# Attention on TensorE: the order of transposes and products with the values, one group at a time and two at a time

## The chip, the cores and the metric

One core of one Trainium2 chip runs the whole program. The metric is the device time of one execution in microseconds (us). TensorE does matmuls and transposes, ScalarE copies and exponentials, VectorE the softmax arithmetic, GpSimd (POOL) elementwise sums, and SyncE (SP) issues the DMA transfers.

## What is computed

A decoder layer over 1024 positions: a convolution group, an attention group and an RWKV-7 group share one input projection; one output projection and a gated MLP follow. The change lies in the attention, which has 8 query heads (2 key/value heads, 4 queries each), 128 queries at a time, and three branches. Cut to the two that matter here:

```python
def one_block(c):                       # 128 queries
    ...
    s = jnp.einsum('bqgrd,bgqnld->bgrqnl', qc, kg).astype(f32) * scale
    ps = masked_softmax(s, msel, (-2, -1))
    o_sel = jnp.einsum('bgrqnl,bgqnld->bqgrd', ps.astype(vg.dtype), vg)
    ...
    s = jnp.einsum('bqgrd,bkgd->bgrqk', qc, kwc).astype(f32) * scale
    pw = masked_softmax(s, mwin, (-1,))
    o_win = jnp.einsum('bgrqk,bkgd->bqgrd', pw.astype(vwc.dtype), vwc)
    return gc[..., 0:1] * o_cmp + gc[..., 1:2] * o_sel + gc[..., 2:3] * o_win
```

The third branch, `o_cmp`, attends to compressed blocks and is small.

## The kernel before

The kernel is traced in program order and a planner then orders the instructions of every engine ahead of time: earlier work of the program goes first when it is ready in the planner's own timeline, later work fills the gaps. Each engine then runs its list strictly in that order and waits for semaphores.

`attn_tile(i)` handles one tile of 128 queries; eight tiles run in the order 7, 6, 5, 4, 0, 3, 2, 1. For each of two branches (`br` 2 is the window of up to 640 keys, `br` 1 is all keys up to the tile's last, under the selection mask) and each of four heads `r` (two key/value heads `g` at once) it does this:

- scores, L897 and L898: a high and a low part of the keys, in pieces of at most 512 keys, into a PSUM bank of the tag `mm` (3 banks);
- L901 adds the mask and takes the minimum (VectorE), into a buffer `pp` (6 of them); L908 the exponential (ScalarE); L909, L910 and L915 the scale by the reciprocal sum and the gate (VectorE);
- then in groups of up to 256 keys: up to four transposes of 128 x 128 (L922) into a PSUM bank of the tag `tr` (2 banks); one copy of the bank to a buffer `pT` by ScalarE (L925); up to four products with the values (L930), each for one key/value head, into 64 of the 128 partitions of the tile's accumulator `av` (1 bank).

After the window branch `cmp_av` adds the compressed branch (L866, L868, L869); at the end L936 copies `av` out and L937 stores it. Beside the attention run the RWKV chain (`rwkv_chain`, L595, L601, L612, L615), which the program gives a high priority, sums of the MLP's down weights on POOL (L949 to L952), and towards the end the load and splitting of the output projection's weights (`wout_load`, L968, L971, with `split` at L120 and L121). Behind it comes the output projection (`out_tile`, matmuls at L229, loads at L988 and L992).

## Time and profile before

| | us |
|---|---|
| median of 3 runs | 1487.43 |
| the runs | 1487.43, 1487.57, 1479.73 |
| the profiled execution | 1479.4 |
| its span, first to last instruction | 1477.5 |
| the attention's stretch in it | 396.0 to 704.5 |

In the views below a row of the timeline is: start in us, length in us, engine, line, operation, out<-in, form (rows and columns of the array, then partitions x elements), count, and in brackets the idle time of the engine before it with what ended it. PE is TensorE's matmuls, PEld its weight loads, DVE VectorE, ACT ScalarE. Matmuls are pipelined, so the lengths of neighbours overlap: what one costs is read from start to start.

### The profile page before, as it was taken

To read this page: it belongs to the slowest core of one execution; us is meant where nothing else is said; L and a number is where in the kernel's file an instruction comes from. 1 tells how busy PE (TensorE), PEld (TensorE's weight loads), DVE (VectorE), ACT (ScalarE), POOL (GpSimd) and SP (SyncE) were. 2 spreads that over 40 slices of the span, in tenths; PEclk is the share of its full clock that TensorE was granted. 3 is DMA by queue.
4 is the path that set the end of the run, shared out by engine and by line. 5 is a ranking of instruction groups with operands and counts; after the bars stand their busy time and mean duration, and the time that the engine had idled before them with its cause. 6 is when DMAs were issued, how large, how long until landed. Compare 5 with 4: busy or idle time off the path is not lost.

```text
span 1477.5 us, 22767 instructions
## 1 busy us (share of the span) xinstructions
PE 1388.7 (94%) x7897; PEld 1095.2 (74%) x7897; DVE 1002.7 (68%) x2187; ACT 686.9 (46%) x1377; POOL 499.2 (34%) x607
## 2 busy tenths in 40 slices
PE   6999589998899999999799899999999999999997
PEld 5887457776677676766588677888788788888886
DVE  6347594454868778798257867676775776666685
ACT  5441245624456665678223533343343333445463
POOL 1002996921144066220000144443444442113310
PEclk9999888999899999999899999999999999999999
DMA  6133133436514254542722123332332334986533
GB/s 185 40 107 82 44 103 111 142 84 179 153 33 139 78 154 125 181 150 81 240 89 83 43 93 93 108 107 70 104 113 93 108 100 162 388 280 216 188 92 114
DMA packets 206679, 186.69 MB, mean 126 GB/s; under 512 B 56355, under 2 KB 145764, under 8 KB 206564
## 3 DMA queue, kind: packets, MB, share of 16 engines
q1 hardware_dynamic: 206564, 185.24, 40.3%
q8 instruction: 62, 1.02, 0.3%
q14 instruction: 53, 0.43, 0.1%
HBM read 126.99 MB, written 58.20 MB: 125 GB/s over the span
## 4 chain that ended last, share of the span: by engine, by line
PE 79%; DVE 8%; POOL 4%; DMA 3%; ACT 2%; issue 2%; SPq 1%; ACTq 0%; DVEq 0%; POOLq 0%
PE gb L229 13%; PE mm L229 12%; PE rw L229 10%; PE ga L229 9%; PE gc L229 8%; PE tr L229 5%; PE tr L922 5%; PE av L930 4%; PE mm L897 2%; PE mm L898 2%; POOL sT L534 1%; POOL sx L532 1%; DVE pp L901 1%; POOL cacc L279 1%; DVE pp L915 1%
## 5 line engine op out<-in xcount | busy, mean ns | idle before, releaser
L229 PE MATMUL mm<-hT,whi 128*128 128x512 f32 x608 | 200.3, 409 | 19.6 <-DVE ev L690 14.8
L229 PEld LDWEIGHTS mm<-hT,whi 128*128 128x128 f32 x608 | 115.7, 193 | 48.9 <-ACT whi L120 20.2
L229 PE MATMUL mm<-hT,wlo 128*128 128x512 f32 x304 | 123.0, 407 | 1.9 <-DVE wlo L121 1.9
L925 ACT ACTIVATE pT<-tr 128x512 f32<-128x512 f32 (+1 forms) x152 | 79.9, 536 | 60.6 <-PE tr L922 59.2
L930 PE MATMUL av<-pT,V 128*64 128x128 f32 x1056 | 96.0, 287 | 1.5 <-ACT pT L925 1.5
L1076 POOL TENSOR_TENSOR S<-wraw,wr 128x512 f32<-128x512 f32 x22 | 28.5, 1296 | 192.8 <-DVE or L107 91.1
L922 PE MATMUL tr<-idn,pp 128*128 128x128 f32 x528 | 90.3, 289 | 1.8 <-DVE pp L915 1.8
L279 POOL TENSOR_TENSOR cacc<-cacc,ctap 128x512 f32<-128x512 f32 x60 | 85.1, 1429 | 12.7 <-ACT ctap L278 12.4
L121 DVE TENSOR_TENSOR sp<-rb,sp 128x512 fp32r<-128x512 f32 x66 | 55.6, 842 | 49.4 <-ACT sp L120 49.4
L229 PE MATMUL rw<-woh,mix 128*128 128x512 f32 x240 | 79.5, 407 | 9.0 <-ACT mix L120 9.0
L229 PE MATMUL rw<-sp,sp 128*128 128x512 f32 x330 | 86.0, 389 | 0.0
L229 PE MATMUL tr<-sp,sp 128*128 128x512 f32 x330 | 85.9, 389 | 0.0
L897 PE MATMUL mm<-KH,QS 128*128 128x512 f32 (+2 forms) x192 | 77.7, 411 | 3.1 <-DVE mx L901 2.8
L930 PEld LDWEIGHTS av<-pT,V 128*64 128x64 f32 x1056 | 59.2, 136 | 28.3 <-issue 13.7
L922 PEld LDWEIGHTS tr<-idn,pp 128*128 128x128 f32 x528 | 55.9, 141 | 30.5 <-issue 29.1
L915 DVE TENSOR_SCALAR pp<-pp,sm 128x640 f32<-128x640 f32 (+7 forms) x128 | 76.5, 638 | 0.9
L120 ACT ACTIVATE sp<-rb 128x512 fp32r<-128x512 f32 x66 | 41.6, 630 | 74.1 <-PE tr L229 36.5
L121 DVE TENSOR_TENSOR sp<-b,sp 128x512 fp32r<-128x512 f32 x88 | 72.1, 827 | 5.2 <-ACT sp L120 5.0
L229 PEld LDWEIGHTS mm<-hT,wlo 128*128 128x128 f32 x304 | 58.5, 193 | 18.1 <-DVE wlo L121 3.8
L229 PEld LDWEIGHTS tr<-sp,sp 128*128 128x128 f32 x330 | 61.9, 188 | 12.9
L229 PEld LDWEIGHTS rw<-sp,sp 128*128 128x128 f32 x330 | 61.9, 188 | 12.9
L532 POOL TENSOR_TENSOR sx<-sN,sT 128x60 f32<-128x60 f32 (+24 forms) x124 | 48.0, 387 | 63.0 <-DMA sN<-dn 54.9
(455 smaller groups left out, 3648.8 us busy)
## 6 DMA issues: line engine op xcount, KB each, us to landing
wr<-in_ffn_w_gate_dram SPq DMA_DIRECT2D x44, 256.0 KB
wraw<-in_ffn_w_up_dram SPq DMA_DIRECT2D x44, 256.0 KB
pdS<-prod SPq DMA_DIRECT2D x44, 256.0 KB
b<-pdS SPq DMA_DIRECT2D x44, 256.0 KB
rb<-tdT SPq DMA_DIRECT2D x44, 256.0 KB
pdA<-prod SPq DMA_DIRECT2D x33, 256.0 KB
b<-pdA SPq DMA_DIRECT2D x33, 256.0 KB
wraw<-in_w_in_dram SPq DMA_DIRECT2D x30, 256.0 KB
```

Source lines behind the costliest of these rows:

```text
L120: self.nc.scalar.activation(hi, src, AF.Copy)
L121: getattr(self.nc, eng).tensor_tensor(lo, src, hi.bitcast(F32), op=ALU.subtract)
L229: mm = lambda l, r, **k: self.nc.tensor.matmul(out, l, r, skip_group_check=more, **k)
L279: nc.gpsimd.tensor_tensor(t[:, o:o + 512], t[:, o:o + 512], z, op=ALU.add)
L532: v_.tensor_tensor(x, N[:, q, q + 1:32].unsqueeze(2).to_broadcast([P, n, w]), Tm[:, q, 0:w].unsqueeze(1).to_broadcast([P, n, w]), op=ALU.mult)
L897: pe.matmul(pts[g][:, 0:n], QS[:, r, g, :], KH[g][hf][:, ks], start=True, stop=False)
L898: pe.matmul(pts[g][:, 0:n], QS[:, r, g, :], KL[g][hf][:, ks], start=False, stop=True)
L915: v.tensor_scalar(Ps[g], Ps[g], sm[:, g:g + 1], None, op0=ALU.mult)
L922: pe.transpose(pt[:, o:o + P], Ps[g][:, kt * P:kt * P + P], self.idn)
L925: s.activation(pT[:, 0:n], pt[:, 0:n], AF.Copy)
L930: pe.matmul(av[g * 64:g * 64 + 64, r * P:r * P + P], self.V[kk // 2][:, kk % 2, vo + g * 64:vo + g * 64 + 64], pT[:, o:o + P], start=first ...
L1076: gp.tensor_tensor(t, x, y, op=op)
```

## The change

Products are no longer traced behind the evacuation of their own group. They are put on a list; when the list holds two groups, the products of both are traced. `issue_after(x)` puts the TensorE instructions traced in its block behind `x` in TensorE's queue: an order of issue, no wait for `x` to finish. The products stand behind the last transpose of the second group, and every group's transposes stand behind the last product traced before them (`av_ins`, kept across tiles). The list is emptied at the end of a tile. What is computed, and the number of instructions, stays the same.

```diff
         first = [True, True]
+        pend = []
+        after = lambda ins: self.tc.issue_after(ins) if ins is not None else nullcontext()
+
+        def products():
+
+            for br, r, lo_k, W, vo, kts, pT, ti in pend:
+                with after(pend[-1][-1]):
+                    for kt in kts:
+                        kk = lo_k // P + kt
+                        for g in range(2):
+                            o = (kt - kts[0]) * 256 + g * P
+                            self.av_ins = pe.matmul(av[g * 64:g * 64 + 64, r * P:r * P + P],
+                                                    self.V[kk // 2][:, kk % 2, vo + g * 64:vo + g * 64 + 64], pT[:, o:o + P],
+                                                    start=first[g], stop=br == 1 and r == 3 and kt == W // P - 1).ins
+                            first[g] = False
+            del pend[:]
...
                     pt = self.bank("tr")
-                    for kt in kts:
-                        for g in range(2):
-                            o = (kt - k2) * 256 + g * P
-                            pe.transpose(pt[:, o:o + P], Ps[g][:, kt * P:kt * P + P], self.idn)
+                    with after(self.av_ins):
+                        for kt in kts:
+                            for g in range(2):
+                                o = (kt - k2) * 256 + g * P
+                                t = pe.transpose(pt[:, o:o + P], Ps[g][:, kt * P:kt * P + P], self.idn)
                     pT = self.xt([P, 512], "pT")
                     n = len(kts) * 256
                     s.activation(pT[:, 0:n], pt[:, 0:n], AF.Copy)
-                    for kt in kts:
-                        kk = lo_k // P + kt
-                        for g in range(2):
-                            o = (kt - k2) * 256 + g * P
-                            pe.matmul(av[g * 64:g * 64 + 64, r * P:r * P + P], self.V[kk // 2][:, kk % 2, vo + g * 64:vo + g * 64 + 64], pT[:, o:o + P],
-                                      start=first[g], stop=br == 1 and r == 3 and kt == W // P - 1)
-                            first[g] = False
+                    pend.append((br, r, lo_k, W, vo, kts, pT, t.ins))
+                    if len(pend) == 2:
+                        products()
             if br == 2:
                 cmp_av()
+        products()
```

In `build`, `self.av_ins = None` is set ahead of the loop over the tiles.

## Rows read from the trace of the kernel before

**Rows 1.** The page: each engine's busy time, share of the span, instructions.

```profile
PE 1388.7 (94%) x7897; PEld 1095.2 (74%) x7897; DVE 1002.7 (68%) x2187; ACT 686.9 (46%) x1377; POOL 499.2 (34%) x607
```

**Rows 2.** Stretch table: length, busy us (count) by engine, granted clock, DMA share, GB/s.

```profile
396.00:704.50 308.50, 299.46 (x2720) 217.09 (x2718) 251.09 (x862) 204.59 (x477) 109.58 (x185) 0.99 0.39 117
```

**Rows 3.** The same table, six slices of 20 us: two of them, their sum.

```profile
560.00:580.00 20.00, 17.71 (x140) 13.02 (x142) 19.45 (x65) 11.86 (x28) 11.51 (x17) 0.93 0.43 111
...
660.00:680.00 20.00, 20.00 (x171) 13.82 (x169) 18.00 (x68) 15.65 (x43) 1.02 (x2) 1.00 0.27 79
sum 120.00, PE 116.52 PEld 81.61 DVE 112.90 ACT 84.77 POOL 36.98; mean PE 19.42 PEld 13.60 DVE 18.82 ACT 14.13 POOL 6.16
```

**Rows 4.** Groups by line, attention: count, busy us, mean ns, idle before.

```profile
L930 PE MATMUL av<-pT,V 128*64 128x128 f32 x1056 | 96.0, 287 | 1.5 <-ACT pT L925 1.5
L922 PE MATMUL tr<-idn,pp 128*128 128x128 f32 x528 | 90.3, 289 | 1.8 <-DVE pp L915 1.8
L925 ACT ACTIVATE pT<-tr 128x512 f32<-128x512 f32 (+1 forms) x152 | 79.9, 536 | 60.6 <-PE tr L922 59.2 <-POOL sx L532 1.0
```

**Rows 5.** Timeline of TensorE's matmuls in the attention.

```profile
399.31 0.60 PE L930 MATMUL av<-pT,V 128*64 128x128 f32 x7
...
657.88 0.66 PE L922 MATMUL tr<-idn,pp 128*128 128x128 f32 x4
658.29 0.42 PE L897 MATMUL mm<-KH,QS 128*128 128x384 f32 x1
...
658.82 0.66 PE L930 MATMUL av<-pT,V 128*64 128x128 f32 x8
...
660.35 0.44 PE L601 MATMUL rw<-VA,KB 128*64 128x128 f32 x4
...
662.09 0.66 PE L922 MATMUL tr<-idn,pp 128*128 128x128 f32 x4
...
703.11 0.66 PE L930 MATMUL av<-pT,V 128*64 128x128 f32 x8 [0.27 <-ACT pT L925]
```

**Rows 6.** Weight loads' waits, 396 to 704.5: us in total, times, longest us.

```profile
PEld tr L922 <- issue: 29.1, 144, 1.5
PEld av L930 <- issue: 13.7, 60, 0.4
PEld av L930 <- ACT pT L925: 6.1, 15, 0.8
```

**Rows 7.** Chain of waits: start us, us, what, count.

```profile
522.40 1.02 PE tr L922 x8
...
695.28 1.02 PE av L930 x16
...
699.31 0.59 PE tr L922 x4
699.90 0.59 PE av L930 x8
```

**Rows 8.** Timeline of ScalarE, 652 to 663 us.

```profile
652.64 0.63 ACT L120 ACTIVATE woh<-wraw 128x512 fp32r<-128x512 f32 x1 [0.81 <-DMA wraw<-in_w_out_dram]
...
659.34 0.58 ACT L925 ACTIVATE pT<-tr 128x512 f32<-128x512 f32 x1
...
662.84 0.60 ACT L925 ACTIVATE pT<-tr 128x512 f32<-128x512 f32 x1
```

**Rows 9.** Timeline of TensorE where the output projection begins.

```profile
706.95 0.71 PE L229 MATMUL rw<-woh,mix 128*128 128x512 f32 x1 [3.19 <-ACT mix L120]
...
725.87 0.79 PE L229 MATMUL rw<-woh,mix 128*128 128x512 f32 x1 [5.81 <-ACT mix L120]
```

**Rows 10.** Timeline of TensorE at its longest standstill in the attention.

```profile
577.44 0.80 PE L897 MATMUL mm<-KH,QS 128*128 128x512 f32 x1 [2.29 <-DVE mx L901]
```

**Rows 11.** Stretch table as in rows 2: two stretches with different granted clocks.

```profile
522.00:524.00 2.00, 2.00 (x18) 1.80 (x16) 2.00 (x8) 0.81 (x2) 2.00 (x3) 1.00 0.32 124
...
578.00:579.00 1.00, 1.00 (x4) 0.77 (x3) 0.93 (x5) 0.41 (x1) 0.00 (x0) 0.50 0.07 27
```

More of the change, by code (lines that the diff above doesn't have):

```diff
@@ L1 @@
-from contextlib import ExitStack
+from contextlib import ExitStack, nullcontext
 import numpy as np
@@ L1330, in build @@
         self.nd, self.td = 0, {}
+        self.av_ins = None
         for n, i in enumerate(order):
```

## The prediction

> **What bounds the kernel now.** I began with the page: TensorE has matmuls in flight for 94% of the span, VectorE is busy 68%, ScalarE 46% [rows 1]. These are averages over stages, so the next view was the table of stretches. The change touches only the attention, which runs from 396.0 to 704.5 us; in those 308.5 us TensorE is busy 299.5, VectorE 251.1, ScalarE 204.6, at a granted clock of 0.99 [rows 2]. The stage is TensorE's, with VectorE close behind: in six of its twenty-microsecond slices VectorE is busy 18.0 to 19.5 of 20 (440 to 460, 560 to 600 and 620 to 680; the least, the most and the sum are shown) [rows 3].
>
> Busy is not the same as productive. The groups of the stage by line show 528 transposes, 1056 records of the products with the values (two records for each product, 528 products) and 152 evacuations of a transposed group by ScalarE [rows 4]. The timeline shows their order: a group of transposes, mostly a score matmul or two, then the products of an earlier group, and again [rows 5]. The form stands in each row: a transpose and a score matmul use the array as 128\*128, a product as 128\*64. The waits of the weight loads show what that costs: before 144 visits of transposes the load sat idle with nothing left to wait for but the array, 29.1 us, about 0.2 us each; before products another 13.7 us in 60 [rows 6]. I therefore read the chain of waits for the same work with and without the change of form. Alternating, four transposes take 0.59 us and eight product records 0.59; eight transposes in a row take 1.02, sixteen product records 1.02 [rows 7]. So the second group in a row costs 0.43 instead of 0.59, for either kind.
>
> **The price of a visit, and the rule behind it.** Two groups alternating: 4 x 0.59 = 2.36 us. Two groups paired: 1.02 + 1.02 = 2.04. One visit of products less saves 0.32 us of TensorE. The Trainium skill, page "TensorEngine Tiling (Array Packing)", section Tiling Modes, says that changing the tiling mode, not merely the tile, drains the engine. The trace agrees with it, at 0.2 us of idle weight load for each return to the transposes [rows 6].
>
> **The change, part by part.** No instruction is added or removed. It draws two kinds of edges on TensorE's queue: products wait in the queue behind the second group's transposes, and the next pair's transposes behind these products. Nothing on SP, POOL or the DMA queues is moved by hand; the planner places everything else around it.
>
> 1. *Fewer visits.* Along the timeline of the stage I count 148 runs of 128\*64 work with products in them, the first at 399.31, the last at 703.11 [rows 5]; only four hold more than one group's worth. Afterwards 152 groups make 76 pairs (each tile of 128 queries has four heads in each branch, so the number of groups is even, and no pair stays half full). 148 - 76 = 72 visits less, 72 x 0.32 = 23.0 us. This is the ceiling.
>
> 2. *Company lost.* The RWKV chain also uses 128\*64 (L595, L601, L612, L615), and 26 of the 148 visits share their change of form with it; others stand alone, as at 660.35 [rows 5]. With half as many visits about half of these meetings are lost: 11 x 0.32 = -3.5 us, bounds 0 and -8.3 (all 26).
>
> 3. *Pairs split.* The edges forbid transposes between the two products, not a score matmul. When the second evacuation isn't ready, the planner may put a score in between, and the visit is paid again. The trace of before has no such pair. Bounds: none, or half of 76 (-12.2). Today the product starts a group or more after its own transposes, so most are ready; I take one in eight, 10 x 0.32 = -3.2 us.
>
> 4. *VectorE's ceiling.* The six slices leave VectorE 120.0 - 112.9 = 7.1 us [rows 3]. An even share of the remaining 16 us would be 6.3 there. Work that depends on TensorE cannot fill an engine to the brim; I let half of it go: -3 us, bounds 0 and -6.
>
> 5. *The new wait.* This is the term I know least. The products of a pair wait for ScalarE, and behind them in the in-order queue stand the next transposes, on which VectorE's free buffers and ScalarE's next evacuation depend. The evacuation is 0.60 us and can start 0.09 after its transposes (662.09 + 0.66, then 662.84) [rows 5, 8]. From the first transpose of a pair: 0.66 + 0.09 + 0.60 = 1.35 until the first products may go, while the eight transposes hold TensorE for only 1.02 [rows 7]; the second evacuation follows at about 1.9, the first products end at about 1.85. With nothing in between TensorE idles some 0.3 us a pair, which is all that the pair saves. What covers it is the score matmuls: 0.53 us for a piece of 384 keys (658.29 to 658.82), and a pair's worth of keys has two pieces or more [rows 5]. If ScalarE is held by something else, the cover is too short: it waits 0.81 us for a DMA at 652.64, and the evacuation of the transposes of 657.88, done at 658.54, starts at 659.34 behind an exponential and a copy [rows 5, 8]. Today 7.6 us in all go to products waiting for ScalarE on the two TensorE rows [rows 4, 6]. Bounds: 0, and 76 x 0.32 = -24 if nothing ever covers (more if ScalarE is late as well: the slower rival). I take one pair in six at 0.3: 13 x 0.3 = -4 us, nearer the good end because the rows of before put a score behind nearly every group.
>
> Sum: 23.0 - 3.5 - 3.2 - 3 - 4 = 9.3 us. Behind the attention nothing is gained or lost by itself: the output projection waits for the last evacuation (3.19 us) and then for a load (5.81 us), both hung on the attention's end [rows 9], so they move with it. The profiled execution took 1479.4 us (span 1477.5 and 1.9 around it), giving 1470.1. The three timed runs stand at 1479.73, 1487.43 and 1487.57, so two of three are 8 us above the profiled one, for a reason that one profile cannot show; by these the same gain gives 1478.1. I forecast the middle, 1474.
>
> **The rivals.**
>
> *A: the new wait decides (slower), 0.18.* Each pair now exposes a round trip to ScalarE. For it: 0.3 us idle without cover, and ScalarE's in-order queue also holds exponentials and copies that wait themselves, 0.81 us in one row [rows 8]. Against it: the even spread of score matmuls. It turns the sum as soon as the mean stall is over 13.3 / 76 = 0.17 us a pair (13.3 being the sum without term 5). At 0.9 us (0.3, and 0.6 of another ScalarE instruction in front, by the 0.60 of an evacuation) in 40% of the pairs, 27 us, it gives 13.3 - 27 = 14 us slower: 1493 to 1501.
>
> *B: VectorE becomes the bound, or the planner splits the pairs (no change), 0.28.* For the first: the six slices, and the 2.29 us in which TensorE waits at 577.44 while VectorE is busy [rows 3, 10]. With term 4 at -6 and term 3 at -12 the sum falls to 23 - 3.5 - 12 - 6, about 1.5 us: 1478 to 1486. That the change doesn't do what it says is this case at its end: products adjacent in the program, parted on the engine.
>
> *C: the clock falls, 0.02.* After TensorE stood still before 577.44 the granted clock is 0.50, the lower of its two levels (1.2 GHz) [rows 10, 11]. If pairs of transposes brought that about, the 76 second groups alone would cost 0.43 us more each, 33 us. Against it: the eight transposes in a row at 522.40 ran in a stretch with the clock at 1.00 [rows 7, 11]. The Trainium skill, page "TensorE: Matmul & The Clock Gate", Part 4, states that transposes do not count as activity for the clock; by that, longer runs of them should bring it down, and this trace does not show it.
>
> **How the numbers follow.** Forecast (gain of 5 to 20 us) 0.52; A 0.18, B 0.28, C 0.02. Measurements of this kernel tell about 0.5%, 7.4 us, from no change. The forecast's lower end falls under that bound and B's upper tail over it, and I set them against each other: faster 0.52, same 0.30, slower 0.18. The range runs from 1459 (nearly the ceiling, from the lower level) to 1491 (where A begins at the upper level), leaving out most of A and C and a little below.
>
> **What would show it.** In the trace of after: about 76 to 100 visits of products instead of 148, most with sixteen records in about 1.02 us; the weight loads' idle time before transposes falling from 29.1 us to about 16; TensorE's work in the attention shorter by some 17 us. Right for term 5: products waiting for ScalarE below 15 us; wrong, and A, if that row grows past 20 us. B shows as products in runs of eight with scores between, or as VectorE at 19 of 20 us throughout while the stage stays as long. The forecast is also wrong if the time saved before 704.5 reappears as a longer wait at the start of the output projection.

## The result, and the profile after

The changed kernel takes 1497.56 us (median of 6, 1490.51 to 1498.34) beside 1486.14 us for the kernel before (median of 6, 1479.73 to 1487.57): a ratio of 1.0086, 95% interval 1.0061 to 1.0111. It is slower by 11 us in the medians and by 13 by the ratio; the forecast was 1474 us, 13 us less than the median known then. The profiled execution took 1493.21 us, its span is 1491.4 us at a mean granted clock of 0.966, where before had 1477.5 at 0.971. The lines have moved: transposes L939, evacuation L942, products L883, scores L913 and L914, mask L917, scale L931, sums on POOL L963 to L966.

The page hardly shows it. Busy time by engine, to be read beside [rows 1]:

```profile
PE 1391.0 (93%) x7897; PEld 1103.6 (74%) x7897; DVE 1001.0 (67%) x2187; ACT 684.8 (46%) x1377; POOL 500.8 (34%) x607
```

The stretch of [rows 2] shows where it is. Columns as there:

```profile
396.00:704.50 308.50, 288.12 (x2603) 214.69 (x2602) 245.80 (x831) 191.33 (x446) 106.53 (x183) 0.98 0.37 111
```

In the same 308.5 us TensorE does 117 matmuls fewer (2603 for 2720) and is busy 288.1 instead of 299.5 us. It has gaps it did not have. The weight loads' waits say which, to be read beside [rows 6]:

```profile
PEld tr L939 <- issue: 17.8, 82, 1.1
PEld mm L913 <- DVE mx L917: 10.1, 22, 0.9
PEld av L883 <- ACT pT L942: 9.2, 25, 1.2
PEld av L883 <- issue: 9.0, 31, 1.5
PEld rw L635 <- DVE gyc L632: 7.5, 2, 6.0
...
PEld tr L939 <- DVE pp L931: 2.7, 3, 1.2
```

The row that the change was to shrink did shrink: the drains ahead of transposes fall from 29.1 us to 17.8. What rose is not ScalarE (6.1 to 9.2) but VectorE: scores that wait for a mask to free their bank, the RWKV chain's L635, transposes that wait for scaled scores, 20.3 us together. In before the first and the last of these were 3.5 and 0.8 us, and L635 did not wait; here are the two rows, in the same view of before, not shown earlier:

```profile
PEld mm L897 <- DVE mx L901: 3.5, 4, 2.5
...
PEld tr L922 <- DVE pp L915: 0.8, 1, 0.8
```

Summed over all rows of this view, the weight loads' waits for VectorE grow from 7.4 to 28.2 us, and those of TensorE's matmuls themselves from 4.6 to 17.5. The idle time with nothing left to wait for but the array falls from 54.7 to 38.0 us, and the waits for ScalarE go from 14.8 to 12.9.

**The pair works where it forms.** Timeline of TensorE, one whole pair: sixteen records of products, then the eight transposes. Each costs 1.02 us in the chain of waits, as in [rows 7]:

```profile
441.16 1.09 PE L883 MATMUL av<-pT,V 128*64 128x128 f32 x16
442.18 1.09 PE L939 MATMUL tr<-idn,pp 128*128 128x128 f32 x8
```

**But nearly half of the pairs are split.** A visit is a run of 128\*64 work with products in it. TensorE's timeline has 149 visits before and 111 after (the expectations below count 112), not 76 to 100. Only 26 visits hold sixteen records; 45 hold eight. Of the 76 pairs 35 are parted: in 25 a score matmul stands between the halves, in ten other work, six times the compressed branch's transposes. The planner lets in what is ready in its timeline while the second evacuation is not; when the second group goes first (below), no pair is parted. The next fence begins with one such pair.

**And TensorE stands still for 5.7 us once.** Timeline of TensorE, 464 to 477 us:

```profile
464.18 0.66 PE L883 MATMUL av<-pT,V 128*64 128x128 f32 x8
464.77 0.45 PE L913 MATMUL mm<-KH,QS 128*128 128x384 f32 x1
465.05 0.34 PE L914 MATMUL mm<-KL,QS 128*128 128x384 f32 x1
465.32 0.44 PE L883 MATMUL av<-pT,V 128*64 128x128 f32 x4
465.69 1.09 PE L939 MATMUL tr<-idn,pp 128*128 128x128 f32 x8
472.51 1.12 PE L635 MATMUL rw<-idn,gyc 128*128 128x128 f32 x4 [5.73 <-DVE gyc L632]
473.56 2.07 PE L640 MATMUL rw<-lora,lw_w 64*128 64x512 f32 x2
475.56 1.98 PE L883 MATMUL av<-pT,V 128*64 128x128 f32 x16
```

L635 belongs to the RWKV chain. It waits for L632 on VectorE, and everything behind it in TensorE's in-order queue waits with it. Timeline of VectorE in the same time:

```profile
464.56 0.15 DVE L925 RECIPROCAL sm<-sm 128x2 f32<-128x2 f32 x1
464.64 1.22 DVE L922 TENSOR_TENSOR nm<-mx 128x2 f32<-128x2 f32 x1
...
465.86 1.23 DVE L926 TENSOR_TENSOR sm<-sm,gates 128x2 f32<-128x2 f32 x1
...
467.13 3.26 DVE L931 TENSOR_SCALAR pp<-pp,sm 128x896 f32<-128x896 f32 x2
470.31 1.22 DVE L115 TENSOR_TENSOR rs_t<-rs_t,rs_h 128x8 f32<-128x8 f32 x1
...
471.76 0.69 DVE L632 TENSOR_TENSOR gyc<-gyc,gr 128x512 f32<-128x512 f32 x1
...
472.56 0.16 DVE L926 TENSOR_TENSOR sm<-sm,gates 128x2 f32<-128x2 f32 x1
```

The same L926, two by 128 numbers, takes 1.23 us at 465.86 and 0.16 at 472.56. What differs is the neighbour. Timeline of POOL, the first and the last of the five instructions between:

```profile
464.57 1.27 POOL L963 TENSOR_TENSOR wraw<-whi,wraw 128x512 f32<-128x512 f32 x1
...
469.99 1.52 POOL L966 TENSOR_TENSOR wraw<-wraw,wlo 128x512 f32<-128x512 f32 x1
```

Each of the VectorE instructions of 1.2 us ends with the POOL instruction beside it, to 0.03 us (464.64 + 1.22 = 465.86, on POOL 464.57 + 1.27 = 465.84). In before the same sums met the same engine, but behind the chain's step: L632 ran ahead of them, and L635 followed without a wait. Three rows of before, not shown earlier; the timeline of VectorE:

```profile
454.63 0.69 DVE L632 TENSOR_TENSOR gyc<-gyc,gr 128x512 f32<-128x512 f32 x1
```

TensorE:

```profile
456.92 0.60 PE L635 MATMUL rw<-idn,gyc 128*128 128x128 f32 x4
```

And POOL, the first of the sums:

```profile
459.03 1.73 POOL L949 TENSOR_TENSOR wraw<-whi,wraw 128x512 f32<-128x512 f32 x1
```

The clock falls with the standstill. Stretch table of after, columns as in [rows 2], two stretches with the granted clock at 0.51, the lower of its levels:

```profile
390.00:400.00 10.00, 10.00 (x44) 8.41 (x44) 7.13 (x29) 2.33 (x5) 1.04 (x1) 0.51 0.11 18
471.50:478.50 7.00, 5.99 (x28) 3.82 (x28) 4.10 (x10) 1.03 (x2) 0.01 (x1) 0.51 0.19 49
```

In the second, the pair at 475.56 takes 1.90 us to the next start instead of 1.02. The first lies where TensorE's queue holds the same 1911 matmuls in the same order in both kernels, ahead of the first transposes; before had 1.00 there, and its first transposes start 6.0 us earlier (396.17, here 402.14). A stretch at the lower level begins there, between 359 and 369 us, in all twenty traces of this study; it lasts 14 to 21 us in fifteen, 31 in one and 34 in four (this one and three of the experiments below, one of which took no longer than before). So 6 us of the difference between these two profiles precede the changed work, and nothing here shows that the change causes them.

**The books.** I added up TensorE's intervals from start to start, from the attention's first score to the 1201st matmul of L229 (inside the output projection, the same point in every kernel). The usual interval between two kinds of instruction is the first quartile of all such intervals at full clock in six traces. What a kernel's order adds up to at these is "order"; the excess in stretches at the lower level, up to half the time, is "clock"; the rest is "waits". Only differences mean something.

| us | total | order | clock | waits |
|---|---|---|---|---|
| before | 360.8 | 261.9 | 10.2 | 88.7 |
| after | 375.3 | 252.9 | 18.1 | 104.2 |
| after less before | +14.4 | -9.0 | +7.9 | +15.5 |

The order is shorter, as the change means it to be, by 9.0 us. It is paid back with 23.4. The books price an interval by its two instructions alone, so a part of each change of form is counted as waits; by the price of a visit worked out below, the order is shorter by some 11 us instead of 9, and the waits are longer by the difference.

### The profile page after: what moved, and what is told of

It is laid out like the page before. It is cut to its first block, busy times and chain, and to the rows that moved or that the text cites. A ratio compares the mean times of both kernels' runs of the same rounds, so it can differ in the third digit from the quotient of the medians.

```text
span 1491.4 us, 22752 instructions
## 1 busy us (share of the span) xinstructions
PE 1391.0 (93%) x7897; PEld 1103.6 (74%) x7897; DVE 1001.0 (67%) x2187; ACT 684.8 (46%) x1377; POOL 500.8 (34%) x607
## 3 DMA queue, kind: packets, MB, share of 16 engines
q8 instruction: 62, 1.02, 0.3%
## 4 chain that ended last, share of the span: by engine, by line
PE 76%; DVE 12%; POOL 4%; DMA 3%; issue 2%; ACT 2%; SPq 1%; ACTq 0%; DVEq 0%
PE gb L229 12%; PE mm L229 12%; PE rw L229 11%; PE ga L229 9%; PE gc L229 8%; PE tr L229 5%; PE av L883 3%; PE tr L939 3%; DVE pp L917 2%; DVE pp L931 2%; PE mm L913 2%; POOL sT L534 1%; PE mm L914 1%; POOL sx L532 1%; POOL cacc L279 1%
## 5 line engine op out<-in xcount | busy, mean ns | idle before, releaser
L229 PE MATMUL mm<-hT,whi 128*128 128x512 f32 x608 | 200.7, 410 | 19.7 <-DVE ev L690 14.9
L229 PEld LDWEIGHTS mm<-hT,whi 128*128 128x128 f32 x608 | 116.0, 194 | 49.0 <-ACT whi L120 20.3
L229 PE MATMUL mm<-hT,wlo 128*128 128x512 f32 x304 | 123.2, 407 | 1.9 <-DVE wlo L121 1.9
L942 ACT ACTIVATE pT<-tr 128x512 f32<-128x512 f32 (+1 forms) x152 | 75.8, 534 | 58.5 <-PE tr L939 57.5
L883 PE MATMUL av<-pT,V 128*64 128x128 f32 x1056 | 87.1, 286 | 3.8 <-ACT pT L942 3.6
L279 POOL TENSOR_TENSOR cacc<-cacc,ctap 128x512 f32<-128x512 f32 x60 | 86.1, 1446 | 11.2 <-ACT ctap L278 11.1
L229 PE MATMUL rw<-sp,sp 128*128 128x512 f32 x330 | 86.2, 389 | 0.0
L229 PE MATMUL tr<-sp,sp 128*128 128x512 f32 x330 | 85.9, 389 | 0.0
L913 PE MATMUL mm<-KH,QS 128*128 128x512 f32 (+2 forms) x192 | 79.6, 420 | 6.0 <-DVE mx L917 4.5
L229 PE MATMUL rw<-woh,mix 128*128 128x512 f32 x240 | 78.2, 401 | 6.7 <-DVE xn L1012 6.7
L939 PE MATMUL tr<-idn,pp 128*128 128x128 f32 x528 | 78.7, 284 | 2.9 <-DVE pp L931 2.8
L883 PEld LDWEIGHTS av<-pT,V 128*64 128x64 f32 x1056 | 58.3, 137 | 26.5 <-ACT pT L942 11.3
L939 PEld LDWEIGHTS tr<-idn,pp 128*128 128x128 f32 x528 | 57.5, 142 | 22.8 <-issue 19.1
L924 ACT ACTIVATE pp<-pp,nm 128x640 f32<-128x640 f32 (+3 forms) x64 | 57.7, 905 | 33.5 <-DVE nm L922 33.5
L931 DVE TENSOR_SCALAR pp<-pp,sm 128x640 f32<-128x640 f32 (+7 forms) x128 | 72.0, 602 | 1.0
L229 PEld LDWEIGHTS mm<-hT,wlo 128*128 128x128 f32 x304 | 58.7, 193 | 18.2 <-DVE wlo L121 3.8
L229 PEld LDWEIGHTS rw<-sp,sp 128*128 128x128 f32 x330 | 61.9, 188 | 13.1 <-DVE sp L121 0.3
L229 PEld LDWEIGHTS tr<-sp,sp 128*128 128x128 f32 x330 | 61.9, 188 | 12.9
```

The source lines that it names most:

```text
L229: mm = lambda l, r, **k: self.nc.tensor.matmul(out, l, r, skip_group_check=more, **k)
L279: nc.gpsimd.tensor_tensor(t[:, o:o + 512], t[:, o:o + 512], z, op=ALU.add)
L883: self.av_ins = pe.matmul(av[g * 64:g * 64 + 64, r * P:r * P + P], self.V[kk // 2][:, kk % 2, vo + g * 64:vo + g * 64 + 64], pT[:, o:o + P ...
L913: pe.matmul(pts[g][:, 0:n], QS[:, r, g, :], KH[g][hf][:, ks], start=True, stop=False)
L924: s.activation(Ps[g], Ps[g], AF.Exp, bias=nm[:, g:g + 1], scale=-1.0, accum_out=sm[:, g:g + 1])
L931: v.tensor_scalar(Ps[g], Ps[g], sm[:, g:g + 1], None, op0=ALU.mult)
```

## The experiments

The expectations name the theories by letters. W: the edges take away TensorE's freedom to run ahead, and it waits. V: the pairs are split, so too few visits are saved. E: the round trip to ScalarE decides (rival A). D: VectorE's load decides. L: this one plan places some instruction badly. P: the price of a change of form can't be redeemed at all. T: TensorE is the bound, and what is taken from it arrives. C: POOL's sums meet VectorE's instructions and hold TensorE's queue through them. "Ratio" is always to the kernel before, with its 95% interval; the median of before beside it is of the same chip and session.

**The edges without the pairs.**

```diff
-                    if len(pend) == 2:
+                    if len(pend) == 1:
                         products()
```

> The list holds one group instead of two: every group's transposes stand behind the products of the group before, and no products are put together. Theory W (waits): in the changed kernel the joined visits pay, but the edge on the transposes takes TensorE's run-ahead away, and TensorE then stands in its queue for ScalarE and VectorE. Here run-ahead is smaller still and nothing is saved, so W expects clearly slower than the kernel before, 1505 to 1540 us against 1486, with TensorE's waits for evacuations and for VectorE grown by 20 us or more. Theory V (visits): what is lost is that pairs are split and the merge saves too little; order of issue itself is harmless; V expects the time of before, 1482 to 1490. Theory L (placement): the loss is one standstill of the RWKV chain's end and a stretch at the lower clock that happened to fall so; L expects anything within 10 us of before.

1548.93 us beside 1481.58, ratio 1.0467 (1.0418 to 1.0515), with 152 visits for 149. The number of visits is nearly that of before; what is gone is the freedom to put the next group's transposes ahead of this group's products. Waits of all engines, 396 to 780 us, in the profiled execution, the slowest of the four (1561.83 us):

```profile
DVE pp L917 <- PE tr L939: 48.1, 31, 6.3
PEld av L883 <- ACT pT L942: 39.1, 56, 3.4
```

VectorE waits for buffers that transposes would have freed, TensorE for the evacuation. Running ahead is worth 67 us to this kernel, three times the 23 us that were to be had from visits. Two groups at a time give nearly all of it back, not all.

**One edge alone.**

```diff
-                    with after(self.av_ins):
+                    with nullcontext():
                         for kt in kts:
```

> The changed kernel without its edge on the transposes; the products keep theirs. In the queue this gives 151 visits, as before (149): it is the edge on the transposes that makes the pairs. If gain and loss both hang on it, the time is that of the kernel before, within 4 us; if the products' edge costs something by itself, it is 5 us or more slower.

1480.6 us, ratio 0.9971 (0.9941 to 1.0001), 150 visits. Products that only stand behind the second group's transposes cost nothing and join hardly any: the planner lets the next group's transposes in between. The edge on the transposes makes the pairs, and the loss comes with it.

**Pairs that are not split.** The products of the second group go first. When its evacuation is done, so is the first group's, and nothing can come between:

```diff
-            for br, r, lo_k, W, vo, kts, pT, ti in pend:
+            todo, z = pend[::-1], (pend or [[0]])[-1]
+            final = z[0] == 1 and z[1] == 3 and z[5][-1] == z[3] // P - 1
+            for br, r, lo_k, W, vo, kts, pT, ti in todo:
...
-                                                    start=first[g], stop=br == 1 and r == 3 and kt == W // P - 1).ins
+                                                    start=first[g], stop=final and pT is todo[-1][6] and kt == kts[-1]).ins
```

> The pair's second group is multiplied first. Its evacuation is the later one, so once the first product may go the other three or more may go too, and nothing gets between: the queue holds 76 visits instead of 112 in the changed kernel. Theory V: 36 visits less at 0.28 us (10.6 us for 38 visits in the accounting of the two traces) take 10 us off the changed kernel: 1485 to 1489, no faster than before. Theory W: the merge pays the same 10 us, but the first products now wait for both evacuations, 0.3 us or more a pair: 10 - 76 x 0.3 = 13 us slower than the changed kernel at worst, so 1492 to 1510. Theory L: within 10 us of the changed kernel either way.

1480.76 us beside 1481.58, ratio 0.9996 (0.9981 to 1.001). Now all 76 visits are whole, and the time is that of before, lower than the 1485 to 1489 that V had expected. By the same books as above its order is 13.1 us shorter than that of before, its waits 10.2 longer and its time at the lower clock 5.1. Weight loads' waits, 396 to 704.5 us:

```profile
PEld tr L941 <- issue: 17.2, 85, 0.8
PEld mm L915 <- DVE mx L919: 16.2, 29, 1.9
PEld av L885 <- ACT pT L944: 12.5, 24, 1.9
```

Split pairs (V) are a part of the loss, then, but mending them gains nothing over before: the score matmuls now wait 16.2 us for VectorE's masks, where they waited 3.5.

**Pairs that never wait for ScalarE.** Each pair's products go one pair later, behind the next pair's transposes (`cmp_av` then waits until the window branch's products are out):

```diff
-        pend = []
+        pend, owed = [], []
...
-            for br, r, lo_k, W, vo, kts, pT, ti in pend:
+            for br, r, lo_k, W, vo, kts, pT, ti in pend[0:2]:
...
-            del pend[:]
+            del pend[0:2]
+            if owed and not any(p[0] == 2 for p in pend):
+                owed.pop()()
...
-                    if len(pend) == 2:
+                    if len(pend) == 4:
                         products()
...
-                cmp_av()
-        products()
+                owed.append(cmp_av)
+        while pend:
+            products()
```

> Pairs are kept, but one pair later: products of groups 1 and 2 stand behind the transposes of groups 3 and 4, and the transposes of 5 and 6 behind these products (the compressed branch follows when the last window products are out). 82 visits in the queue. TensorE now has a pair of transposes (1.02 us) between a group's transposes and its products, as before the change. Theory W: the merge pays (149 - 82) x 0.28 = 19 us and the waits of the changed kernel mostly go: 1466 to 1478. Theory V: the merge pays the same 19 us, so V expects 1466 to 1478 as well; what tells V from W is the pair of this run and rev. Theory L: 1477 to 1497.

1484.84 us, ratio 1.0025 (1.0001 to 1.005), 82 visits; W and V had both expected 1466 to 1478. Weight loads' waits in the same stretch; no row of products waiting for ScalarE is left in it:

```profile
PEld tr L941 <- issue: 15.6, 42, 3.5
PEld mm L915 <- DVE mx L919: 12.9, 14, 4.5
...
PEld tr L941 <- ACT pT L944: 3.7, 9, 1.0
```

The products' round trip to ScalarE (E) is gone, and nothing is gained. It does not decide alone. Transposes now wait 3.7 us for evacuations, and the scores wait for VectorE all the same. One more buffer for the transposed groups, which this order holds longer:

```diff
-  pT=5
+  pT=6
```

> As late, with six buffers pT for evacuated groups instead of five: four groups on the list, one for the compressed branch, one to spare. 78 visits. If buffers hold late back, this is faster than late by 2 to 8 us (1462 to 1474); if not, within 3 us of it.

1488.73 us, ratio 1.0053 (1.0033 to 1.0072), 78 visits, scores waiting 17.4 us for masks. The buffer was not what held it.

**More room, or less work, for VectorE's side.** Seven score buffers instead of six (paid with one of the query buffers), in before and in the whole pairs:

```diff
-  pp=6, q8=2
+  pp=7, q8=1
```

> The kernel before with seven buffers for the scores of a head instead of six (and one buffer instead of two for a small load). If the number of heads in flight is no limit there, within 4 us of the kernel before.

> rev with the same buffers. If the held transposes cost time because they give buffers back to VectorE later (its masks waited 12.2 us for transposes in rev, 8.0 before), one more buffer takes 5 us or more off rev and not off the kernel before: 1466 to 1476. If not, within 4 us of rev's 1481.

1485.69 us, ratio 1.001 (0.9985 to 1.0035), and 1495.4 us, ratio 1.0079 (1.005 to 1.0109). The exchange does nothing for before and harms the pairs; whether by the buffer given, by the one taken or by the new plan is not shown. Half of the scaling moved from VectorE to ScalarE, in the whole pairs:

```diff
-  sc=0
+  sc=1
```

> rev, complete, with the scaling of the first value head's exponentials on ScalarE instead of VectorE (L915's other branch; 38 of its 76 us leave VectorE, about as much comes to ScalarE, which is busy 204 of 308 us). Theory C: half of VectorE's longest instructions leave the port that POOL blocks, so rev improves by 4 to 15 us: 1466 to 1477. Against it: ScalarE's evacuations, on which each pair waits, queue behind more work; then 1481 to 1495.

1488.34 us, ratio 1.0025 (1.0004 to 1.0046), where C had expected 1466 to 1477: a miss. Then the scaling left out altogether, in three kernels:

```diff
-                for g in range(2):
-                    if g < self.B["sc"]:
-                        s.activation(Ps[g], Ps[g], AF.Copy, scale=sm[:, g:g + 1])
-                    else:
-                        v.tensor_scalar(Ps[g], Ps[g], sm[:, g:g + 1], None, op0=ALU.mult)
```

> The kernel before with VectorE's scaling of the exponentials (L915, 76 us of VectorE in the attention) left out, so its output is not the reference's; the base for the next two. Both theories: TensorE has matmuls in flight for 299 of 308 us, so the base itself gains little, 1462 to 1480 us, mostly from the few waits for VectorE (577.44 and 511.36) and the first steps of the lower clock.

> The changed kernel with the same scaling left out; 115 visits. Theory D: the changed kernel's 11 us of loss turn into a gain of 2 to 10 us against before_noscale. Theory E: the loss stays, 6 to 14 us slower than before_noscale.

> rev (second group's products first, 76 visits) with the same scaling left out. Theory D: rev gained 15 us of TensorE work against before, and gave it back in waits for VectorE (a score matmul waiting for a PSUM bank: 1.3 us before, 6.5 in rev) and in the lower clock that follows them; with 76 us less on VectorE the gain must show: 10 to 18 us less than before_noscale. Theory E: it was given back in the round trip to ScalarE (a product waiting for an evacuation: 0.9 us before, 6.6 in rev) and in run-ahead; then VectorE's work is no matter and rev_noscale stays within 4 us of before_noscale.

1467.91 us, ratio 0.9869 (0.9832 to 0.9906); 1474.87, 0.9938 (0.9905 to 0.9971); 1475.03, 0.9927 (0.9895 to 0.996), all beside 1484.93. Without the scaling the pairs still lose 7 us to single groups. These three say less than they seem to: up to the attention's first score the profiled before_noscale is already 6 us ahead of the other two (373.7 us against about 379.8), and the kernels do the same work up to there. Inside the attention the three profiles differ by about 2 us. D had expected the pairs to gain 2 to 18 us over before_noscale. With less load on VectorE the changed kernel's loss is small, but no gain appears; whether load alone is the matter is not settled by these.

**Is TensorE's time worth anything?** Products for both value heads at once, in the form 128\*128, so that no form changes between transposes and products; half of the products is left out with that:

```diff
-                        for g in range(2):
-                            o = (kt - k2) * 256 + g * P
-                            pe.matmul(av[g * 64:g * 64 + 64, r * P:r * P + P], self.V[kk // 2][:, kk % 2, vo + g * 64:vo + g * 64 + 64], pT[:, o:o + P],
-                                      start=first[g], stop=br == 1 and r == 3 and kt == W // P - 1)
-                            first[g] = False
+                        o = (kt - k2) * 256
+                        pe.matmul(av[:, r * P:r * P + P], self.V[kk // 2][:, kk % 2, vo:vo + 128], pT[:, o:o + P],
+                                  start=first[0], stop=br == 1 and r == 3 and kt == W // P - 1)
+                        first[0] = False
```

> The kernel before without the change of form at the products: each of a group's products uses all 128 columns of the array (both value heads against the transposed weights of the first alone), so half of the products is left out and the output is not the reference's. The stream of columns stays as long as it was (two such products one behind the other instead of two pairs side by side), the order of work stays as before, and the drain on both sides of a visit is gone. Theory P (the price can't be redeemed: when TensorE gets faster, the queues of an order fixed ahead of time make it wait elsewhere instead): 149 x 0.28 = 42 us of TensorE's time go, and less than 15 us of it reaches the end: 1468 to 1482. Theory T (TensorE bounds the stage and the edges are what costs): most reaches the end, 1440 to 1460.

> The changed kernel with the same products: the edges and pairs stay, but there is no drain left for them to save. What this differs from before_full is the cost of the edges alone. Theory T: 11 us net loss and 10 us gain in the changed kernel mean that the edges cost about 20 us: 16 to 26 us slower than before_full. Theory P: TensorE has time to spare without the drains, and the edges cost under 8 us.

1473.78 us beside 1482.83, ratio 0.9939 (0.9918 to 0.9961), and with the edges of the change 1465.93, ratio 0.9891 (0.985 to 0.9931). The edges, with no drain left for them to save, make this kernel 8 us faster (the intervals just overlap), where T had expected 16 to 26 us slower and P a cost under 8. So in that kernel the edges cost nothing by themselves, and two plans of the same work differ by 8 us, not much less than what the change lost. In the chain of before_full the drains are gone:

```profile
644.32 0.44 PE av L929 x4
644.77 0.44 PE tr L922 x4
```

A group's transposes and products cost 0.44 + 0.44 instead of 0.59 + 0.59 [rows 7], 0.30 us less. The runs of 128\*64 work in TensorE's timeline fall from 172 to 47, as the RWKV chain's remain. By this estimate 125 x 0.30 = 37 us are taken from the engine that is busy 97% of the stage. 9 us arrive, a quarter. This is the most telling run of the study: the premise that time saved on TensorE arrives is wrong by a factor of four. A part goes to the clock: between 440 and 760 us the lower level holds for 27 us in this trace, 17 in before. The weight loads' waits of before_full, 396 to 704.5 us, show what came instead:

```profile
PEld av L929 <- ACT pT L925: 12.4, 17, 2.1
PEld mm L897 <- DVE mx L901: 9.0, 15, 2.8
PEld rw L635 <- DVE gyc L632: 6.1, 3, 4.8
PEld tr L922 <- issue: 5.6, 14, 0.8
```

And it has the changed kernel's standstill, though it has no edge and no pair. TensorE's timeline of before_full:

```profile
468.61 1.12 PE L635 MATMUL rw<-idn,gyc 128*128 128x128 f32 x4 [4.58 <-DVE gyc L632]
```

POOL's five sums lie from 461.02 to 468.01 in it, right in front. The standstill is therefore no property of pairs. At this step of the chain five traces have L635 waiting more than 0.6 us: these two, after_full (2.81), before with seven buffers (2.66) and the whole pairs (0.96). In all five the step L632 is planned behind the start of POOL's sums. That is not enough for it: in late L632 comes at 463.76, the first sum at 459.81, and L635 does not wait. Nor does the standstill rank the kernels. Before with seven buffers is level with before, and the whole pairs with seven buffers have no such wait and are slower by 0.8%.

**POOL's sums left out.** In four kernels:

```diff
-        tt(b[0, 0], b[0, 1], b[0, 0], op=ALU.subtract)
-        tt(b[0, 1], b[1, 1], b[0, 1], op=ALU.subtract)
-        tt(b[1, 1], b[1, 1], b[0, 0], op=ALU.subtract)
-        tt(b[1, 0], b[1, 0], b[1, 1], op=ALU.subtract)
```

> The kernel before with POOL's sums of the down weights left out (its loads and stores stay; the output is not the reference's); the base for the next two. Theory C (the meeting of POOL and VectorE): VectorE's instructions in the attention that take over 0.15 us more than usual, all beside a POOL instruction, add up to 27 us before; without the sums most of that goes, and the base gains 3 to 12 us: 1470 to 1480. If VectorE's delays are all hidden, within 3 us of before.

> The changed kernel with the same sums left out. Theory C: the loss of 11 us was that meeting (5.4 us of standstill and the lower clock behind it, 3.4 us, and smaller ones), so it goes: 8 us faster to 2 us slower than before_nosums. Theory P (the queues' fixed order makes TensorE wait elsewhere for what it saves, whatever POOL does): still 6 to 14 us slower.

> Products in the form of the whole array (half of them left out, no drains) and POOL's sums left out. If TensorE bounds the stage once VectorE is undisturbed, the 42 us of drains are redeemed in good part: 25 to 40 us below before_nosums. If another engine's turn comes at once, under 15 us below it, as with the sums (9 us).

> rev (76 visits) with POOL's sums left out, against before_nosums at 1470.2. If only the split pairs of the changed kernel eat the gain, 73 visits less at 0.28 us are 20 us, and half of it or more arrives: 1450 to 1460. If what is saved is lost in the round trip to ScalarE (the first product waits for the second evacuation), 1464 to 1474.

| | us | ratio | interval | the same with the sums |
|---|---|---|---|---|
| before | 1470.22 | 0.9899 | 0.9848 to 0.9949 | 1 |
| after | 1471.86 | 0.9907 | 0.9878 to 0.9936 | 1.0086 |
| whole pairs | 1466.38 | 0.9883 | 0.9849 to 0.9917 | 0.9996 |
| before, no drains | 1449.97 | 0.9754 | 0.9703 to 0.9804 | 0.9939 |

The kernel before gets 1.0% faster without the sums, the changed one 1.8%, and the two are then level. So nearly all of the change's loss goes with POOL's sums (C). With POOL silent the loss is gone but the gain still is not there: by the books after_nosums stands to before_nosums with -6.5 us in the order, -0.2 in the clock and +5.7 in waits; the whole pairs with -15.4, +1.2 and +8.8. The sum of the latter, -5.4 us, shows in the medians as 3.8, inside both intervals. And taking out the drains now gives 20 us instead of 9, of some 36 (167 runs of 128\*64 work become 47): more than half arrives, less than the 25 to 40 us expected if TensorE bounds the stage and more than the 15 if not. Weight loads' waits, 396 to 690 us, of before without the sums:

```profile
PEld tr L922 <- issue: 27.9, 141, 1.5
...
PEld av L930 <- ACT pT L925: 4.8, 13, 0.8
```

The changed kernel without them:

```profile
PEld tr L939 <- issue: 16.9, 84, 0.8
PEld av L883 <- ACT pT L942: 9.6, 24, 1.3
...
PEld mm L913 <- DVE mx L917: 6.1, 14, 0.8
```

Whole pairs without them:

```profile
PEld tr L941 <- issue: 17.8, 85, 0.8
PEld av L885 <- ACT pT L944: 11.1, 22, 1.9
PEld mm L915 <- DVE mx L919: 8.0, 16, 1.1
```

Before without the sums has 0.8 us in the row of the masks. Whole pairs without them lie in the range expected of the round trip to ScalarE (1464 to 1474), but by these rows both waits share it: products wait 11.1 us for ScalarE, scores 8.0 for masks. The idle time saved ahead of transposes is 10 to 12 us with and without POOL's sums; the waits for masks are smaller without it (6.1 for 10.1, 8.0 for 16.2), and the long waits of L635 are gone. The plan is not the same, though: after_nosums has 119 visits, since the planner places its work anew.

**Only the place of the sums.** The first sums come one tile of queries later, and more of them behind the third and fourth tile:

```diff
-  ds=((), (0, 1, 2), (3, 4), (5, 6, 7), (8, 9), (10,), (), ())
+  ds=((), (), (0, 1, 2, 3), (4, 5, 6, 7), (8, 9), (10,), (), ())
```

> rev with the first sums of the down weights started one tile of queries later (four, four, two and one of them behind the third to sixth tile instead of three, two, three, two and one behind the second to sixth). Nothing is left out. Theory C: POOL is idle while the RWKV chain of the first half ends, rev's half-speed stretch at 472 and its 1.1 us there go, 2 to 8 us below rev's 1481: 1473 to 1479. Against it: the sums come denser later and meet VectorE there; then 1479 to 1490.

1491.01 us, ratio 1.0051 (1.0017 to 1.0084), in the whole pairs, where C had expected 1473 to 1479: a miss. L635 no longer waits at that step, and the kernel is slower all the same. Moving the meeting does not remove it; scores wait 21.3 us for masks here.

**One row in all of them.** Weight loads of scores waiting for a mask, 396 to 704.5 us, from the same view of each trace:

| kernel | us, times | ratio |
|---|---|---|
| before | 3.5, 4 | 1 |
| one edge alone | 5.2, 8 | 0.9971 |
| before, seven buffers | 5.3, 7 | 1.001 |
| after | 10.1, 22 | 1.0086 |
| one pair later | 12.9, 14 | 1.0025 |
| whole pairs | 16.2, 29 | 0.9996 |
| the edges without the pairs | 17.0, 21 | 1.0467 |
| one pair later, one buffer more | 17.4, 20 | 1.0053 |
| whole pairs, sums moved | 21.3, 32 | 1.0051 |
| whole pairs, scaling halved | 22.7, 30 | 1.0025 |
| whole pairs, seven buffers | 24.9, 36 | 1.0079 |

In every kernel in which groups are paired it is three to seven times that of before. It grows without pairs too: in the edges without the pairs, and to 9.0 us in before_full, which has no edge. It does not rank the kernels (after has the lowest of the paired ones and the highest time), so it is one of the ways in which the gain goes, not all of it.

## Why the prediction was wrong, point by point

- **What bounds the kernel.** Failed, and the rest follows from it. I read "TensorE busy 299.5 of 308.5" [rows 2] as "time saved on TensorE arrives". Some 37 us of drains taken out gave 9 us, and some 36 gave 20 with POOL silent. By the rows of waits, a shorter order on TensorE makes it wait for VectorE; which buffer carries that wait is not shown (one more of two kinds did not help).
- **The price of a visit, 0.32 us.** Right in size, a little high. At full clock, most often, four transposes take 0.383 us from the first start to the last in before and 0.328 in before_full; eight product records take 0.385, their four 0.332; from the last product to the next transpose it is 0.203 and 0.112. With as much again on the way to the products, that is 0.055 + 0.053 + 2 x 0.091 = 0.29 us a visit. The books make it 9.0 / 38 = 0.24 and 13.1 / 62 = 0.21 (TensorE's timeline has 172 runs of 128\*64 work before, 134 after and 110 in the whole pairs), because a part of it is in their waits. The idle time before transposes went to 17.8 us where about 16 was said.
- **Step 1 and 3, visits and split pairs.** The step that failed by count. One in eight pairs split was said, 10; it was 35. The bound (half of 76) had it; the value taken did not. The argument was that the product starts a group or more after its own transposes in before. That was the run-ahead which the edges then forbid: the trace of before was used as evidence on a freedom that the change removes.
- **Step 2, company lost.** Runs without products are 172 - 149 = 23 before and 134 - 111 = 23 after: nothing lost. In the whole pairs 110 - 76 = 34, the 11 that were said.
- **Step 4, VectorE's ceiling.** The term that was mis-sized most. 3 us, at most 6, was said; the waits of weight loads for VectorE rose by 16.0 us in the three rows (20.3 less 3.5 and 0.8) and by 20.8 in all, those of TensorE's matmuls by 12.9. I had priced a rate, how much more work VectorE could take, and not a meeting: small VectorE instructions stretched by POOL's, in front of an instruction that heads TensorE's queue. [rows 10] showed a standstill of that family (ahead of it VectorE instructions of 128x2 take 1.26 and 1.00 us, at 571.91 and 573.52, beside POOL's sums), and I used it only for rival B.
- **Step 5, the wait for ScalarE.** About right: 4 us were said; the row went from 6.1 to 9.2, and with TensorE's own matmuls from 7.6 [rows 4, 6] to 11.5. Whole pairs that never wait for ScalarE (late) gain nothing.
- **Rival A** named the right side with the wrong engine: the wait that takes the place of the one removed is VectorE's. The 1493 to 1501 us that it gave contain the result, by chance. **Rival B** described what is seen, products in runs of eight with scores between, and held that it would end level.
- **Rival C.** No run shows that transposes lower the clock: eight in a row at 442.18 take 1.09 us at full clock. The clock did fall, behind the standstill at 472 and in the stretch before 400, and costs 7.9 us more than in before. The first follows the standstill; for the second, no run here shows a cause in the change.
- **The output projection.** Nothing reappears there: TensorE's hand-over took 3.19 and 5.81 us before [rows 9] and takes 6.66 once in after, since its first matmuls now run beside the attention's end.

What is shown: the order on TensorE got shorter, and its waits for VectorE grew by more; the loss goes with POOL's sums (11 us in the medians with them, 2 without, where the intervals overlap); whole pairs as such do not lose; no form of pairing gains. What is seen in one execution only: the standstill of 5.7 us with 6.8 us at the lower clock behind it. What stays open: how much of the rest is the change and how much the particular plan, which leaving out the sums changed as well. Small edits to buffers and to the place of the sums moved the whole pairs by 0 to 0.8% without a pattern that I could tie to one row. No kernel that computes all of the reference beats the one before beyond its interval.

## What to carry to other kernels

An engine that is busy 97% is not yet the one that sets the time: take a part of its work out once (here the drains, of which a quarter arrived), and see how much arrives before pricing a rearrangement in that engine's microseconds. A hand-written order in a planned queue removes run-ahead, so the old trace is no witness on how ready the operands will be under the new order. And the in-order queue makes a distant neighbour matter: five elementwise sums on POOL stretched five VectorE instructions, and behind these stood the one that TensorE's next instruction waited for.

## What the runs showed of the hardware

I had not expected how much a POOL instruction costs VectorE. A TENSOR_TENSOR of 128x2 goes from 0.16 to 1.22 us beside a POOL TENSOR_TENSOR of 128x512 (1.27), and two scalings of 128x896 from 0.69 each to 3.26 together; a RECIPROCAL of one input stays at 0.15, as at 662.82 with 1.2 us of a POOL sum still to run. Between 378 and 740 us every VectorE instruction that takes over 0.15 us more than its form usually does lies beside a POOL instruction: 38 in before with 27 us in all, 41 with 31 us in after, and 7 with 2.8 us once the sums are left out. The Trainium skill, page "SBUF — State Buffer", section "SBUF: two separate sides", says that VectorE and GpSimd share a pair of ports as an exclusive lock for the whole instruction, "not a bandwidth split", for VectorE instructions with two inputs in SBUF or in certain modes. The trace agrees, with 1.22 us for 0.16; that the wait then reaches TensorE through its queue, 5.73 us at 472.51, is this kernel's own doing.
